# The second MLP product by Strassen's seven products instead of eight, in a two-layer hybrid decoder trunk

## Chip and metric

One core of a Trainium2 chip runs the whole program. The metric is device microseconds of one execution, median of the runs shown.

## What is computed

Two layers (DEPTH = 2) act on 512 tokens of 1024 features. Each layer normalises x, makes one wide input projection, runs three token mixers on its column groups (stick-breaking attention, sparse attention with a top-k indexer, a gated linear recurrence), merges them by sigmoid gates, projects the sum and adds it to x. Then comes the MLP:

```python
h2 = rms_norm(x, norm_mlp[l])
x = x + jnp.square(jax.nn.relu(h2 @ w_up[l])) @ w_down[l]
```

w_up is 1024 x 4096 and w_down is 4096 x 1024, all in float32.

## The kernel before

Activations lie with features on the 128 partitions and the 512 tokens along the free axis, so x is eight tiles of 128 x 512. Every main product is made in three passes for accuracy: each operand is cut into a high part (a copy in the reduced float32r format) and a low part (the remainder), and TensorE adds high x high, high x low and low x high into one PSUM bank. For weights, `split_weights` makes the high part on ScalarE and the remainder on VectorE, from a raw block of 1024 x 256 that one DMA on SP's queue has loaded into one of two raw buffers (N_RAW). High and low parts of weights have five buffers each (N_W); all activations share 76 tiles (N_T).

`fm` makes one output tile of 128 features: for each k-tile of 128 it issues the three matmuls of 512 columns. The MLP of a layer runs in four groups of 1024 hidden features. In group g the first product makes eight tiles u: `take_u` evicts a bank on VectorE with max(., 0) and the norm's factor, ScalarE squares it twice (into the high part and in place), VectorE makes the remainder. The second product (`rows_to_res`) takes 1024 rows of w_down in four column blocks of 256, that is two output tiles of eight k-tiles each, and `take_res` adds each finished bank to its tile of x on VectorE. In the last group `done` norms each x tile for the next layer (`norm_tile`) or sends it out.

The order of all instructions is fixed when the program is built. Operations are recorded first, each with a lane (main, prep for weights, norm, and one for each mixer: sb, idx, dsa, hg), a level and a planned duration; `order` then plays them forward on five engines. `choose` takes for each engine the ready operation with the earliest planned start and then the smallest level; AHEAD limits how far beyond the oldest open operation of a lane it may look; `of_banks` and `of_tiles` limit which lane may take a PSUM bank or a tile. ORDER_IN is the order of the input projection's column groups (h0 to h3, hv for the recurrence; iq and the tail of sv for the indexer; sqk and sv for the attention; dq for the sparse attention), ORDER_MIX the order in which the mixers are recorded, ORDER_OUT that of gates and branch projections. On the chip each engine runs its list in order.

In the profile nearly all engine operations carry the line of a helper: L586 for matmuls, L592 for transposes, L522 for everything on VectorE, ScalarE and GpSimd, L609 for DMAs. The tiles tell them apart: wr is a raw weight block, wh and wl its high and low parts, u, uh and ul the MLP's activations, pm the bank of a main product, zs and pi banks of the attention and the indexer.

Of the kernel before, what the change touches and what calls it, by code (L numbers as in the profile page):

```python
# [7 lines left out]
F32 = mybir.dt.float32  # L8
# [3 lines left out]
AF = mybir.ActivationFunctionType  # L12
# [4 lines left out]
P = 128  # L17
# [4 lines left out]
DEPTH = 2  # L22
# [19 lines left out]
LV_GATE = 1  # L42
SMALL = ("var", "rtok", "iw", "m8", "dss", "drs", "mn", "sm", "rc", "dec", "hrs")
ROOM = {"main": 12}
AHEAD = {"dsa": 80, "hg": 64, "idx": 160, "sb": 50}
BANKS = 4
BRANCHES = ("sb", "dsa", "hg")
ORDER_IN = ("h0", "h1", "h2", "h3", "hv", "iq", "sqk", "sv", "dq")
ORDER_MIX = ("sb", "index", "hgrn", "dsa_inputs", "dsa")
ORDER_OUT = (("gate", "sb", 0), ("gate", "sb", 1), ("gate", "dsa", 0), ("gate", "dsa", 1), ("branch", "sb", 0),  # L50
             ("gate", "hg", 0), ("gate", "hg", 1), ("branch", "dsa", 0), ("branch", "sb", 1), ("branch", "dsa", 1),
             ("branch", "hg", 0), ("branch", "hg", 1))
LEVELS = (4, 8, 16, 32)

# [160 lines left out]
class Program:  # L215
# [100 lines left out]
    def order(self, caps):  # L316
# [24 lines left out]
        avail = {e: [] for e in ENGINES}  # L341
# [5 lines left out]
        done, worked = [], {}  # L347
# [31 lines left out]
        def choose(e):  # L379
            c = clock[e]  # L380
            pick = None
            for o in avail[e]:
                if o.ready + SLACK[e] > c and pick is not None and pick[0][0] <= o.ready + SLACK[e]:
                    if pick[0][0] < o.ready + SLACK[e]:
                        continue
                if o.at - base[o.lane] >= AHEAD.get(o.lane, 1 << 30):
                    continue
                at = may(o)
                if at is None:
                    continue  # L390
                s = max(c, o.ready + SLACK[e], at)
                p = o.prio
                if e == "ACT" and o.acts and acts and o.acts != acts:
                    p = (p[0] + 3, p[1])
                key = (s, p)
                if pick is None or key < pick[0]:
                    pick = (key, o, max(c, o.ready, at))
            return pick

        while len(done) < len(self.ops):  # L400
# [6 lines left out]
            _, _, e = min(live)  # L407
            o, s = best[e][1], best[e][2]
# [3 lines left out]
            line, b = lanes[o.lane], base[o.lane]  # L412
            if o.at == b:
                while b < len(line) and line[b].gone:
                    b += 1
                base[o.lane] = b
                if o.lane in AHEAD:
                    stale |= set(ENGINES)
# [8 lines left out]
            us = o.us  # L427
# [4 lines left out]
            if e == "PE":  # L432
# [3 lines left out]
                w = int(s / SPAN)  # L436
# [16 lines left out]
            for t in o.tiles:  # L453
                t.left -= 1
                t.free_at = max(t.free_at, o.end)
                if not t.left and t.tag in free:
                    have = free[t.tag]
# [70 lines left out]
class Kernel:  # L528
# [224 lines left out]
    def tm(self, units, acts, n, consumer, tiles=range(NT)):  # L753

        banks = self.g.gang([self.ps("pm") for _ in tiles])
        k = 0
        for src in units:
            hi, lo = self.split_weights(src)
            c = hi.shape[1]
            self.on("main", 1)  # L760
            for bank, t in zip(banks, tiles):
                self.products(bank[:, 0:n], [(hi[:, i, :], lo[:, i, :]) for i in range(c)],
                              [tuple(x[:, P * t:P * (t + 1)] for x in acts[k + i]) for i in range(c)],
                              k == 0, k + c == ND, True)
            k += c
        self.on("main", 0)
        for bank, t in zip(banks, tiles):
            consumer(bank[:, 0:n], t)


    def begin_norm(self, gain0):
# [435 lines left out]
    def layer(self, l):  # L1207
        V = self.V
        L = {"hq": [], "hf": []}
        self.on("main", 0)  # L1210
        hid = self.hid
# [5 lines left out]
        w = self.w_in[l]  # L1217
# [52 lines left out]
        for s in ORDER_IN:  # L1270
            steps[s]()
        for s in ORDER_MIX:
            getattr(self, s)(L, l)
        self.on("main", 0)
        gates = {}
        mixed = [None] * ND
        final = []
# [19 lines left out]
        def branch(br, half):  # L1297
            wb = {"sb": self.w_sb, "dsa": self.w_dsa, "hg": self.w_hg}[br][l]
            ap = self.rows(wb, 512 * half, 512)
            r = self.load([(None, ap)], list(ap.shape))  # L1300
            for i in range(4):
                m = 4 * half + i
                t = gates.pop((br, m))

                def take_y(ps):
                    o = V.tensor_mul(t, t, ps)
                    if br == BRANCHES[-1] and m == 0:
                        L["late"] = [o]
                    if br == BRANCHES[0]:
                        mixed[m] = t  # L1310
                        return
                    V.tensor_add(mixed[m], mixed[m], t)
                    if br == BRANCHES[-1]:
                        hi, lo = self.r(name="mxh"), self.r(name="mxl")
                        self.split(hi, lo, mixed[m])
                        mixed[m] = None
                        final.append((hi, lo))

                self.fm([r[:, :, P * i:P * (i + 1)]], L["o_" + br], take_y)
# [19 lines left out]
        def rows_to_res(src, acts, after):  # L1339
            for c in range(4):  # L1340
                for j, u in enumerate(self.by_features(src, 256 * c)):
                    m = 2 * c + j
                    self.fm(u, acts, lambda ps: (take_res(ps, m), after(m)))

        rows_to_res(self.w_out[l], final, lambda m: self.norm_tile(m))
        hid = self.hid
        for g in range(4):
            self.on("main", 0)
            us = []

            def take_u(ps):
                t = self.f(name="u")
                V.scalar_tensor_tensor(t, ps, 0.0, self.rbc, op0=ALU.max, op1=ALU.mult)
                hi, lo = self.r(name="uh"), self.r(name="ul")
                self.act(hi, t, AF.Square)
                self.act(t, t, AF.Square)
                V.tensor_sub(lo, t, hi.bitcast(F32))
                us.append((hi, lo))

            for c in range(4):  # L1360
                for u in self.by_features(self.w_up[l], 1024 * g + 256 * c):
                    self.fm(u, hid, take_u)
            last = g == 3 and l + 1 < DEPTH
            if last:
                self.begin_norm(8 * (l + 1))
            def done(m):
                if last:
                    self.norm_tile(m, True)
                elif g == 3:
                    self.dma(self.out[P * m:P * (m + 1), :], self.xT[m])  # L1370

            rows_to_res(self.w_down[l][1024 * g:1024 * (g + 1), :], us, done)

    def run(self):
        V = self.V
# [22 lines left out]
def of_banks(lane, k, have, used, first):  # L1398
    n = lambda *lanes: sum(used.get(("ps", x), 0) for x in lanes)
    if lane == "main":  # L1400
        return n("main") + k <= BANKS
    if lane in ("norm", "out"):
        return True
    if not first or n("sb", "dsa", "idx", "hg") + k > 6:
        return False
    if lane in ("dsa", "idx"):
        return n("dsa", "idx") + k <= (3 if n("sb", "hg") else 6)
    return True
# [50 lines left out]
```

## Time and profile before

| | |
|---|---|
| median of 3 runs | 1719.15 us (1718.8 to 1719.84) |
| profiled execution | 1718.95 us, span of its instructions 1717.2 us |
| busy: TensorE, VectorE, ScalarE | 1675.1, 1025.6, 797.2 us |

The time of an execution is a little longer than the span between the first and the last profiled instruction. Busy times are unions of instructions; an instruction's duration can be longer than the time until the next one starts on the same engine, since they are pipelined.

### The profile page before, as it was taken

Reading aid. Unit: us, or ns where it says so; the run is one execution under the profiler, and the core shown is the slowest. Engines: PE = TensorE matmul, PEld = TensorE weight load, DVE = VectorE, ACT = ScalarE, POOL = GpSimd, SP = SyncE. Lnnn points to the kernel's source line nnn. Section 1 sums busy time; section 2 is a strip of 40 time slices with the busy share of each in tenths; the row PEclk is TensorE's granted clock in tenths of the full one; section 3 lists DMA queues with packets and bytes.
Section 4 is the critical chain, followed back from the end, with each engine's and each line's share of the span. In section 5 each row is a group of like instructions: output and inputs, shape, how many; then the busy total and the mean of one; then the engine's idle time right before and its main releaser. Section 6 shows DMA issues by size and latency. Waiting matters only on the chain.

```text
span 1717.2 us, 22265 instructions
## 1 busy us (share of the span) xinstructions
PE 1675.1 (98%) x8624; PEld 1364.9 (79%) x8624; DVE 1025.6 (60%) x2208; ACT 797.2 (46%) x1498; POOL 20.8 (1%) x12
## 2 busy tenths in 40 slices
PE   7999999998899999999999999999988999999999
PEld 6888887786688888888888888887766888888887
DVE  7545578996765443444564555699968643434342
ACT  6346867336444242324452568563464442424241
POOL 0000010000000000000000001000000000000000
PEclk9999999999999999999999999999999999999999
DMA  6222121220332323322432222212203323232322
GB/s 188 98 93 74 50 74 50 72 83 32 111 102 94 99 98 98 98 98 98 135 111 98 70 81 67 74 44 74 65 29 135 99 98 98 98 99 98 98 98 74
DMA packets 144154, 152.64 MB, mean 89 GB/s; under 512 B 5296, under 2 KB 128688, under 8 KB 144048
## 3 DMA queue, kind: packets, MB, share of 16 engines
q1 hardware_dynamic: 143328, 150.55, 27.0%
q8 instruction: 67, 1.10, 0.3%
q10 hardware_dynamic: 720, 0.68, 0.1%
q14 instruction: 39, 0.32, 0.1%
HBM read 147.02 MB, written 4.19 MB: 88 GB/s over the span
## 4 chain that ended last, share of the span: by engine, by line
PE 92%; DVE 5%; ACT 2%; issue 1%; DMA 0%; ACTq 0%; DVEq 0%
PE pm L586 82%; PE zs L586 3%; PE ph L586 2%; DVE gate L522 2%; PE po L586 1%; PE pd L592 1%; DVE wl L522 1%; PE pi L586 1%; DVE lg L522 1%; PE pd L586 1%; PE pt L592 1%; ACT lg L522 0%; DVE work L522 0%; DMA c2a<-in_cst_dram 0%; DVE mxl L522 0%
## 5 line engine op out<-in xcount | busy, mean ns | idle before, releaser
L522 ACT ACTIVATE wh<-wr 128x512 fp32r<-128x512 f32 (+3 forms) x552 | 336.9, 617 | 719.4 <-PE pm L586 699.3
L522 DVE TENSOR_TENSOR wl<-wr,wh 128x512 fp32r<-128x512 f32 (+3 forms) x552 | 362.0, 669 | 303.5 <-ACT wh L522 195.9
L586 PE MATMUL pm<-hh,wh 128*128 128x512 f32 x1120 | 392.8, 393 | 9.6 <-ACT wh L522 9.6
L586 PE MATMUL pm<-hh,wl 128*128 128x512 f32 x1120 | 395.3, 395 | 0.1
L586 PE MATMUL pm<-hl,wh 128*128 128x512 f32 x1120 | 393.9, 393 | 0.0
L586 PEld LDWEIGHTS pm<-hh,wh 128*128 128x128 f32 x1120 | 211.0, 188 | 52.9 <-ACT wh L522 9.6
L586 PEld LDWEIGHTS pm<-hh,wl 128*128 128x128 f32 x1120 | 210.8, 188 | 44.9 <-issue 1.4
L586 PEld LDWEIGHTS pm<-hl,wh 128*128 128x128 f32 x1120 | 211.0, 188 | 42.9 <-issue 0.5
L586 PE MATMUL pm<-ul,wh 128*128 128x512 f32 x512 | 179.7, 389 | 0.0
L586 PE MATMUL pm<-uh,wl 128*128 128x512 f32 x512 | 179.7, 389 | 0.0
L586 PE MATMUL pm<-uh,wh 128*128 128x512 f32 x512 | 179.7, 389 | 0.0
L522 DVE TENSOR_TENSOR x<-x,pm 128x512 f32<-128x512 f32 x80 | 54.9, 686 | 121.1 <-PE pm L586 120.4
L586 PEld LDWEIGHTS pm<-uh,wl 128*128 128x128 f32 x512 | 96.1, 188 | 20.1
L586 PEld LDWEIGHTS pm<-uh,wh 128*128 128x128 f32 x512 | 96.1, 188 | 19.9
L586 PEld LDWEIGHTS pm<-ul,wh 128*128 128x128 f32 x512 | 96.1, 188 | 19.9
L586 PE MATMUL pm<-wl,hh 128*128 128x512 f32 (+1 forms) x240 | 81.7, 386 | 0.0
L586 PE MATMUL pm<-wh,hl 128*128 128x512 f32 (+1 forms) x240 | 81.7, 388 | 0.0
L586 PE MATMUL pm<-wh,hh 128*128 128x512 f32 (+1 forms) x240 | 81.5, 387 | 0.0
L522 DVE SCALAR_TENSOR_TENSOR u<-pm,rbc 128x512 f32<-128x512 f32 x64 | 44.1, 690 | 57.3 <-PE pm L586 57.3
L522 DVE TENSOR_TENSOR ul<-u,uh 128x512 fp32r<-128x512 f32 x64 | 44.3, 693 | 38.9 <-ACT u L522 38.9
L522 ACT ACTIVATE uh<-u 128x512 fp32r<-128x512 f32 x64 | 40.2, 628 | 31.5 <-DVE u L522 31.5
L586 PEld LDWEIGHTS pm<-wl,hh 128*128 128x128 f32 x240 | 45.1, 188 | 8.2
(218 smaller groups left out, 2091.6 us busy)
## 6 DMA issues: line engine op xcount, KB each, us to landing
wr<-in_w_in_dram SPq DMA_DIRECT2D x42, 1024.0 KB, 5.0
wr<-in_w_up_dram SPq DMA_DIRECT2D x32, 1024.0 KB, 5.4
wr<-in_w_down_dram SPq DMA_DIRECT2D x32, 1024.0 KB, 5.2
wr<-in_w_in_dram SPq DMA_DIRECT2D x16, 512.0 KB, 5.4
wr<-in_w_out_dram SPq DMA_DIRECT2D x8, 1024.0 KB, 5.2
x<-in_x_dram SPq DMA_DIRECT2D x16, 256.0 KB, 5.6
wr<-in_w_in_dram SPq DMA_DIRECT2D x4, 768.0 KB, 4.3
wr<-in_w_br_sb_dram SPq DMA_DIRECT2D x4, 768.0 KB, 4.4
```

The lines of the kernel that those rows point to most:

```text
L522: return self._g.op(self._n, lambda: f(real(out), *[real(a) for a in args], **{k: real(a) for k, a in kw.items()}), outs, ins, us, acts, l ...
L586: return self.g.op("PE", lambda: nc.tensor.matmul(real(out), real(lhsT), real(rhs), start=start, stop=stop, **k), [out], [lhsT, rhs], us, ...
L592: return self.g.op("PE", lambda: nc.tensor.transpose(real(out), real(in_), real(ident)), [out], [in_, ident], us, kind=kind)
```

## The change

The second product is cut into 2 x 2 blocks: the two output tiles of a column block, even and odd k-tiles, and the two halves of 256 tokens. With four weight blocks and four activation blocks, Strassen's method (in Winograd's form) needs seven block products in place of eight, and sums of blocks before and after. `moving_seven` makes four differences for a pair of u tiles and splits seven activation blocks; `seven` makes four weight sums (s1 to s4), splits seven weight blocks, runs seven products of 4 k-tiles x 3 matmuls of 256 columns into three banks (x four times, y once, z twice, in the order x y x z x z x), and after each product adds the bank to one quarter of the two x tiles. All sums are on VectorE. The first column block of group g + 1's first product is recorded ahead of group g's second product. ORDER_IN, ORDER_MIX, ORDER_OUT and AHEAD change, and on TensorE `choose` prefers the oldest main operation that can start by the chosen one's time. SEVEN_OUT is False, so w_out's product stays as it is.

```diff
@@ -42,13 +42,15 @@
 LV_GATE = 1
 SMALL = ("var", "rtok", "iw", "m8", "dss", "drs", "mn", "sm", "rc", "dec", "hrs")
 ROOM = {"main": 12}
-AHEAD = {"dsa": 80, "hg": 64, "idx": 160, "sb": 50}
+AHEAD = {"dsa": 166, "hg": 163, "idx": 160, "sb": 17}
 BANKS = 4
+SEVEN_OUT = False
+LV_MOVE = 2
 BRANCHES = ("sb", "dsa", "hg")
-ORDER_IN = ("h0", "h1", "h2", "h3", "hv", "iq", "sqk", "sv", "dq")
-ORDER_MIX = ("sb", "index", "hgrn", "dsa_inputs", "dsa")
+ORDER_IN = ("sqk", "h0", "h1", "h2", "hv", "h3", "iq", "sv", "dq")
+ORDER_MIX = ("index", "hgrn", "sb", "dsa_inputs", "dsa")
 ORDER_OUT = (("gate", "sb", 0), ("gate", "sb", 1), ("gate", "dsa", 0), ("gate", "dsa", 1), ("branch", "sb", 0),
-             ("gate", "hg", 0), ("gate", "hg", 1), ("branch", "dsa", 0), ("branch", "sb", 1), ("branch", "dsa", 1),
+             ("gate", "hg", 0), ("branch", "sb", 1), ("gate", "hg", 1), ("branch", "dsa", 0), ("branch", "dsa", 1),
              ("branch", "hg", 0), ("branch", "hg", 1))
 LEVELS = (4, 8, 16, 32)
 
@@ -395,6 +397,14 @@
                 key = (s, p)
                 if pick is None or key < pick[0]:
                     pick = (key, o, max(c, o.ready, at))
+            if e == "PE" and pick is not None and pick[1].lane == "main":
+                o = pick[1]
+                for x in avail[e]:
+                    if x.lane == "main" and x.prio < o.prio and x.ready <= pick[2]:
+                        at = may(x)
+                        if at is not None and at <= pick[2]:
+                            o = x
+                pick = (pick[0], o, pick[2])
             return pick
 
         while len(done) < len(self.ops):
@@ -766,6 +776,78 @@
         self.on("main", 0)
         for bank, t in zip(banks, tiles):
             consumer(bank[:, 0:n], t)
+
+
+    def moving_seven(self, b0, b1):
+
+        V = self.V
+        h = lambda a, i: a[:, 256 * i:256 * (i + 1)]
+        ta, tb = self.f(name="ta"), self.f(name="tb")
+        V.tensor_sub(h(ta, 0), h(b0, 1), h(b0, 0))
+        V.tensor_sub(h(ta, 1), h(b1, 1), h(b0, 1))
+        V.tensor_sub(h(tb, 0), h(b1, 1), h(ta, 0))
+        V.tensor_sub(h(tb, 1), h(b1, 0), h(tb, 0))
+        out = {}
+        for src, names in ((h(b0, 0), ("b11",)), (b1, ("b21", "b22")), (tb, ("t2", "t4")), (ta, ("t1", "t3"))):
+            n = 256 * len(names)
+            hi, lo = self.r((P, n), "vh"), self.r((P, n), "vl")
+            self.split(hi, lo, src)
+            for i, k in enumerate(names):
+                out[k] = (h(hi, i), h(lo, i))
+        return out
+
+    def seven(self, src, moving, after):
+
+        V = self.V
+        for c in range(4):
+            ap = self.rows(src, 256 * c, 256)
+            r = self.load([(None, ap)], list(ap.shape)).rearrange("p (k s) c -> p k s c", s=2)
+            a = {(i, j): r[:, :, j, P * i:P * (i + 1)] for i in range(2) for j in range(2)}
+            self.on("prep", 1)
+            s1, s2, s3, s4 = (self.f((P, 4, P), "ws") for _ in range(4))
+            parts = {}
+
+            def cut(k, w):
+                parts[k] = self.split_weights(w)
+
+            cut("a11", a[0, 0])
+            cut("a12", a[0, 1])
+            self.on("prep", 1)
+            self.in_order(V.tensor_add(s1, a[1, 0], a[1, 1]), "last_sum")
+            self.in_order(V.tensor_sub(s2, s1, a[0, 0]), "last_sum")
+            cut("s2", s2)
+            cut("s1", s1)
+            self.on("prep", 1)
+            self.in_order(V.tensor_sub(s3, a[0, 0], a[1, 0]), "last_sum")
+            cut("s3", s3)
+            self.on("prep", 1)
+            self.in_order(V.tensor_sub(s4, a[0, 1], s2), "last_sum")
+            cut("s4", s4)
+            cut("a22", a[1, 1])
+            x = lambda i, j: self.xT[2 * c + i][:, 256 * j:256 * (j + 1)]
+            self.on("seven", 0)
+            banks = {k: self.ps("p" + k) for k in "xyz"}
+            first, order = set(), (("x", "a11", "b11", [(0, 0)]), ("y", "a12", "b21", [(0, 0)]),
+                                   ("x", "s2", "t2", [(0, 1)]), ("z", "s1", "t1", [(1, 1)]),
+                                   ("x", "s3", "t3", [(1, 1)]), ("z", "s4", "b22", [(0, 1)]),
+                                   ("x", "a22", "t4", [(1, 0)]))
+            for bank, w, b, into in order:
+                wh, wl = parts[w]
+                ps = banks[bank][:, 0:256]
+                self.on("main", 1)
+                n = len(moving)
+                for i in range(n):
+                    bh, bl = moving[i][b]
+                    for j, (p, q) in enumerate(((wh, bh), (wh, bl), (wl, bh))):
+                        self.mm(ps, p[:, i, :], q, bank not in first and i == 0 and j == 0, i == n - 1 and j == 2,
+                                skip_group_check=True)
+                first.add(bank)
+                self.on("seven", 0)
+
+                for at in into:
+                    V.tensor_add(x(*at), x(*at), ps)
+            after(2 * c)
+            after(2 * c + 1)
 
 
     def begin_norm(self, gain0):
@@ -1311,6 +1393,10 @@
                         return
                     V.tensor_add(mixed[m], mixed[m], t)
                     if br == BRANCHES[-1]:
+                        if SEVEN_OUT:
+                            if m % 2:
+                                final.append(self.moving_seven(mixed[m - 1], mixed[m]))
+                            return
                         hi, lo = self.r(name="mxh"), self.r(name="mxl")
                         self.split(hi, lo, mixed[m])
                         mixed[m] = None
@@ -1342,34 +1428,38 @@
                     m = 2 * c + j
                     self.fm(u, acts, lambda ps: (take_res(ps, m), after(m)))
 
-        rows_to_res(self.w_out[l], final, lambda m: self.norm_tile(m))
+        (self.seven if SEVEN_OUT else rows_to_res)(self.w_out[l], final, lambda m: self.norm_tile(m))
         hid = self.hid
-        for g in range(4):
-            self.on("main", 0)
-            us = []
-
+        us, moving = {g: [] for g in range(4)}, {g: [] for g in range(4)}
+
+        def up(g, c):
             def take_u(ps):
                 t = self.f(name="u")
                 V.scalar_tensor_tensor(t, ps, 0.0, self.rbc, op0=ALU.max, op1=ALU.mult)
-                hi, lo = self.r(name="uh"), self.r(name="ul")
-                self.act(hi, t, AF.Square)
                 self.act(t, t, AF.Square)
-                V.tensor_sub(lo, t, hi.bitcast(F32))
-                us.append((hi, lo))
-
-            for c in range(4):
-                for u in self.by_features(self.w_up[l], 1024 * g + 256 * c):
-                    self.fm(u, hid, take_u)
-            last = g == 3 and l + 1 < DEPTH
-            if last:
+                us[g].append(t)
+                if len(us[g]) % 2 == 0:
+                    self.on("main", LV_MOVE)
+                    moving[g].append(self.moving_seven(*us[g][-2:]))
+
+            self.on("main", 0)
+            for u in self.by_features(self.w_up[l], 1024 * g + 256 * c):
+                self.fm(u, hid, take_u)
+
+        def done(m):
+            if l + 1 < DEPTH:
+                self.norm_tile(m, True)
+            else:
+                self.dma(self.out[P * m:P * (m + 1), :], self.xT[m])
+
+        for g in range(4):
+            for c in range(1 if g else 0, 4):
+                up(g, c)
+            if g < 3:
+                up(g + 1, 0)
+            elif l + 1 < DEPTH:
                 self.begin_norm(8 * (l + 1))
-            def done(m):
-                if last:
-                    self.norm_tile(m, True)
-                elif g == 3:
-                    self.dma(self.out[P * m:P * (m + 1), :], self.xT[m])
-
-            rows_to_res(self.w_down[l][1024 * g:1024 * (g + 1), :], us, done)
+            self.seven(self.w_down[l][1024 * g:1024 * (g + 1), :], moving[g], done if g == 3 else lambda m: None)
 
     def run(self):
         V = self.V
@@ -1399,8 +1489,10 @@
     n = lambda *lanes: sum(used.get(("ps", x), 0) for x in lanes)
     if lane == "main":
         return n("main") + k <= BANKS
-    if lane in ("norm", "out"):
+    if lane == "norm":
         return True
+    if lane == "seven":
+        return have - k >= 1
     if not first or n("sb", "dsa", "idx", "hg") + k > 6:
         return False
     if lane in ("dsa", "idx"):
```

## Rows read from the trace of the kernel before

**Rows 1.** The page's busy time, share of the span and instructions of each engine.

```profile
span 1717.2 us, 22265 instructions
...
PE 1675.1 (98%) x8624; PEld 1364.9 (79%) x8624; DVE 1025.6 (60%) x2208; ACT 797.2 (46%) x1498; POOL 20.8 (1%) x12
```

**Rows 2.** The page's granted clock in 40 slices, 9 is full speed.

```profile
PEclk9999999999999999999999999999999999999999
```

**Rows 3.** Windows: stretch, then busy us (instructions) by engine, clock, DMA share, GB/s.

```profile
300.00:350.00 50.00, 48.15 (x308) 38.19 (x307) 50.00 (x143) 16.45 (x30) 0.00 (x0) 1.00 0.24 80
400.00:450.00 50.00, 42.44 (x281) 30.30 (x279) 31.47 (x101) 27.30 (x76) 0.00 (x0) 1.00 0.04 12
...
600.00:650.00 50.00, 50.00 (x222) 41.42 (x221) 24.26 (x37) 21.50 (x34) 0.00 (x0) 1.00 0.32 105
```

**Rows 4.** The chain that ended last: start, us, what (two longest pieces).

```profile
523.27 343.89 PE pm L586 x1517
...
1373.99 339.38 PE pm L586 x1497
```

**Rows 5.** Timeline of TensorE in the second product: start, us, instruction, count.

```profile
559.87 0.61 PE L586 MATMUL pm<-uh,wl 128*128 128x512 f32 x2
...
579.36 0.62 PE L586 MATMUL pm<-uh,wh 128*128 128x512 f32 x2
```

**Rows 6.** Timeline of TensorE in two bursts of the mixers, 256 columns.

```profile
136.44 0.28 PE L586 MATMUL zs<-sph,nones 128*128 128x256 f32 x1
136.45 0.19 PEld L586 LDWEIGHTS zs<-spl,nones 128*128 128x128 f32 x1
136.56 0.28 PE L586 MATMUL zs<-spl,nones 128*128 128x256 f32 x1
136.56 0.19 PEld L586 LDWEIGHTS zs<-sph,nones 128*128 128x128 f32 x1
...
136.68 0.22 PE L586 MATMUL zs<-sph,nones 128*128 128x128 f32 x1
...
272.62 0.28 PE L586 MATMUL pi<-ikh,iqT 128*128 128x256 f32 x1
...
272.85 0.40 PE L586 MATMUL pm<-hh,wh 128*128 128x512 f32 x1
```

**Rows 7.** Groups by form: busy us, mean ns of one, idle before and its releaser.

```profile
L522 DVE TENSOR_TENSOR wl<-wr,wh 128x512 fp32r<-128x512 f32 x488 | 329.6, 686 | 298.7 <-ACT wh L522 191.4 <-PE pm L586 106.8
L522 ACT ACTIVATE wh<-wr 128x512 fp32r<-128x512 f32 x488 | 305.5, 631 | 667.9 <-PE pm L586 650.6 <-ACT sq L522 4.0 <-DVE hq L522 4.0
...
L586 PE MATMUL pm<-uh,wl 128*128 128x512 f32 x512 | 179.7, 389 | 0.0
...
L522 DVE SCALAR_TENSOR_TENSOR u<-pm,rbc 128x512 f32<-128x512 f32 x64 | 44.1, 690 | 57.3 <-PE pm L586 57.3
L522 ACT ACTIVATE u<-u 128x512 f32<-128x512 f32 x64 | 40.5, 633 | 2.0
```

**Rows 8.** Timeline of VectorE in the mixers of both layers.

```profile
306.87 1.27 DVE L522 TENSOR_TENSOR wl<-wr,wh 128x512 fp32r<-128x512 f32 x2
308.07 0.68 DVE L522 MAX8 m<-work 128x8 f32<-128x512 f32 x1
...
1015.75 0.42 DVE L522 TENSOR_TENSOR st<-ikw,st 128x256 fp32r<-128x256 f32 x1
1016.09 0.28 DVE L522 SCALAR_TENSOR_TENSOR hst<-hst,f,ph 128x64 f32<-128x64 f32 x1
```

**Rows 9.** Timeline of ScalarE at the start.

```profile
8.96 1.15 ACT L522 ACTIVATE wh<-wr 128x512 fp32r<-128x512 f32 x2 [1.93 <-DMA wr<-in_w_in_dram]
```

**Rows 10.** The page's DMA issues: count, size, median us to landing.

```profile
wr<-in_w_down_dram SPq DMA_DIRECT2D x32, 1024.0 KB, 5.2
```

## The prediction

> **What bounds the kernel now.** I read the busy times first [rows 1]: TensorE is busy for 1675.1 of 1717.2 us, VectorE for 1025.6, ScalarE for 797.2. A busy TensorE need not be at its peak, so the clock comes next: full in all 40 slices [rows 2]. Then the stages [rows 3]: in the MLP (600 to 650 us) TensorE is busy for 50.00 of 50 us and VectorE for 24.26. In the mixers it is otherwise: from 300 to 350 us VectorE is the one with 50.00 of 50, and from 400 to 450 us TensorE is busy for only 42.44. The chain that ended last says the same [rows 4]: two pieces of 343.89 and 339.38 us, one for each layer's MLP, are matmuls and nothing else. So in the MLP a matmul saved is time saved, as long as VectorE, with about half of its time free there, can pay for it.
>
> **TensorE's gain.** The second product now has, for each of 2 layers, 4 groups and 4 column blocks, 2 output tiles x 8 k-tiles x 3 = 48 matmuls of 512 columns: 1536 in all, the 3 x 512 of [rows 7]. In [rows 5] the first and the last of 44 rows of two lie 19.49 us apart: 86 starts, 0.2266 us each. That is 348.1 us. After, a block has 7 products x 4 k-tiles x 3 = 84 matmuls of 256 columns, 2688 in all. Their spacing is seen in short bursts of the mixers [rows 6]: 136.44, 136.56, 136.68, so 0.12 us at two digits, each with a weight load of its own between; another two take from 272.62 to 272.85, 0.115 each. I take the mean, 0.118. 2688 x 0.118 = 317.2 us. The gain is 30.9 us, not the eighth of 348 (43.5), since a 256-column matmul costs 52% of a 512-column one. Taken at 0.116 or 0.12 it would be 36 or 26.
>
> A 256-column matmul leaves 0.118 us to hide a load that lasts 0.19 us in [rows 6]; two loads there start 0.11 us apart and delay nothing. The Trainium skill speaks against the change here: "TensorE: Matmul & The Clock Gate", section "Part 3: Packing small matmuls", says that a weight load overlaps running matmuls only where they use other row groups. All 128 rows of the array are in use here (128*128 in the lines), and yet the load is hidden, so this trace does not agree.
>
> **VectorE's price.** Each VectorE row lasts longer than it holds the engine. In [rows 8] two weight subtractions of 512 start at 306.87 and the next operation at 308.07: 0.60 each, where the mean duration is 0.686 [rows 7]. One of 256 holds it 0.34 (1015.75 to 1016.09). By these:
> A block of the product costs 4 weight remainders and 2 residual adds now, 6 x 0.60 = 3.6 us. After: 7 remainders and 4 weight sums of 512, and 7 adds of 256: 11 x 0.60 + 7 x 0.34 = 9.0 us. A pair of activation tiles costs 2 remainders now, 1.2 us; after, 4 differences and one remainder of 256 and three remainders of 512, 5 x 0.34 + 3 x 0.60 = 3.5 us. With 32 blocks and 32 pairs VectorE holds 32 x 5.4 + 32 x 2.3 = 246 us more. What hides it is TensorE's time in the same stage. For one group, the first product takes TensorE 192 x 0.2266 = 43.5 us, and VectorE 16 x 0.60 (weights) + 8 x 0.60 (evictions) + 4 x 3.5 = 28.4. The second takes TensorE 4 x 9.9 = 39.6 us and VectorE 4 x 9.0 = 36.0. VectorE goes from under half to 78% of the MLP and fits, but in the second product only by 0.9 us a block.
>
> ScalarE: two weight copies take 1.15 us [rows 9] where one lasts 0.631 [rows 7], so 0.52 each; 7 x 0.52 = 3.6 us a block, hidden under 9.9. DMA: the same 32 loads of 1 MB, 5.2 us each [rows 10], on the same queue, one a block of 9.9 us with two buffers; no cost. That the first block of group g+1's first product, with its load and its weight copies, is issued ahead of group g's second product moves work of the same kind, and gives 10.9 us of cover while the last pair of group g is split. The final output DMAs keep their number.
>
> **What is given back.** (a) VectorE runs in order, at 36 of 39.6 us, and gets 2 evictions of the next group besides. Where it comes late, a block stretches. Below, nothing: 3.6 us are left in each group (less than nothing is out, since work is only added). Above, the whole 31 us: then VectorE sets the pace. Of the rows, 300 to 350 us is the nearest, where VectorE is full and TensorE lacks 1.9 us of 50 [rows 3]; I take 1 us for each of the six groups that are followed by another: 6. (b) Group 3 of each layer has no next first product to cover its last pair. After the last matmul come eviction 0.69, square 0.63, copy 0.63, remainder 0.69 [rows 7] before the second of the seven products can use the tile, 2.6 us; TensorE has the first product (1.4 us) and three of four k-tiles of the second (1.1 us). With the differences of the pair behind it I take 1.5 us each: 3 (0 to 8). (c) In the first layer's group 3, eight tiles are normed for the next layer, at two VectorE operations a tile, 16 x 0.60 = 9.6 us upon 36.0, against 39.6: 6 us too much, of which 5 prepared weight parts (3.0 us of remainders) cover half. I take 4 (0 to 8). Together 13.
>
> **The order of the mixers** (input steps, mixer order, look-ahead, oldest main product first). It removes and adds no instruction. From 400 to 450 us TensorE lacks 7.6 us, in 300 to 350 us 1.9 [rows 3]; two layers have each. A better order could win up to about 16 us; widening the recurrence's window moves VectorE work out of 300 to 350 us, where the top-k chain needs it. A worse one can lose as much: the attention's window of 17 operations lets its chain run less far ahead, behind the values that come eighth in the input order, and then its VectorE work falls into that very stretch. Oldest-first gives up 0.25 us of planned slack at some switches. I take 0, with 16 either way.
>
> **Sum.** Against the profiled execution's own 1718.95 us (span 1717.2): 1718.95 - 30.9 + 13 + 0 = 1701. The median of the runs shown, 1719.15, is 0.2 above it, so 1701 it stays.
>
> **Rivals.**
> - *Little comes back.* The planned order keeps VectorE ahead and the mixers win some of their gap: 1719 - 31 + 3 - 6 = 1685. For it: 78% is not 100%. Against it: VectorE is in order and its margin is thin.
> - *The bank's hand-over decides: slower.* Four of seven sums stay in one PSUM bank (x): the next product into it may start only when VectorE has added the last one to the residual, and z has one such turn too: 4 turns a block, 128 in all. Between them lies one product, 12 x 0.118 = 1.42 us. The last matmul goes on for 0.16 us after the next has started (0.28 less 0.12 [rows 6]), the add lasts 0.42 (as the 256-column rows of [rows 8]): with one operation of 0.60 ahead of it that is 1.18 us, and it fits. With two ahead it is 1.78 and TensorE waits 0.36 us, 128 x 0.36 = 46 us: 1719 - 31 + 46 = 1734. It decides from a mean wait of 31/128 = 0.24 us on.
> - *The mixers' order loses.* The gap of 300 to 350 and 400 to 450 us doubles in both layers and 4 more us are given back in the MLP: 1701 + 16 + 4 = 1721; at half of that 1711.
> - *The weights don't hide.* Then each short matmul takes a load more. By rows, 0.118 + 0.11 (the loads' closest spacing, 136.45 to 136.56 [rows 6]) = 0.228, 2688 x 0.228 = 613 us against 348: 1984. That [rows 6] show the loads hidden leaves it 1 in 100. It is what the rule of the Trainium skill's page "TensorE: Matmul & The Clock Gate" named above would do.
> - *No change:* that VectorE sets the pace in the second product (term (a) at its upper end) with the mixers as they are: 1719.
>
> **How the numbers follow.** 0.2% (3.4 us) is about what a measurement of this kernel tells from no change. Chances: forecast 0.43, little comes back 0.25, mixers' order loses 0.14, hand-over 0.13, no change 0.04, weights 0.01. Faster is the first two and under half of the third, 0.74; same the fourth's small cases, the no-change case and part of the third, 0.09; slower 0.17. The likeliest case's own range is 1690 to 1712. The range must hold the first three: 1678 (the full gain, 1688, with 10 of the mixers) to 1722.
>
> **What would show it.** In the profile after: matmuls of 256 columns 0.117 to 0.12 us apart inside a product, with loads between; VectorE's busy share of the MLP's second product near 9 tenths and TensorE's near 10 in the first product; about 83 us for a pair of first and second products (87.0 now). TensorE's idle time before the x and z products, ended by VectorE's residual add, shows the hand-over; idle time ended by weight remainders shows (a); a hole of 1 to 4 us at the last group of each layer (b). The time up to the first MLP matmul of a layer (about 523 us now [rows 4]) shows the mixers' order by itself: it is predicted unmoved. The prediction is wrong if 256-column matmuls are further apart in long runs than in bursts of four, or if VectorE falls behind in its order.

## The result, and the profile after

The changed kernel takes 1672.49 us (median; 1670.55 to 1672.88), the kernel before 1718.97 in the same comparison: ratio 0.9728, 95% interval 0.9711 to 0.9744. That is 46.5 us faster; the forecast was 18, and the range ended at 1678. The profiled execution took 1672.88 us, its span 1671.1.

The page's busy times and the granted clock answer to [rows 1, 2]: VectorE rose from 60% to 76%, the clock stays up.

```profile
span 1671.1 us, 25574 instructions
...
PE 1643.0 (98%) x9776; PEld 1397.6 (84%) x9776; DVE 1272.7 (76%) x2784; ACT 879.9 (53%) x1653; POOL 21.4 (1%) x12
...
PEclk9999999999999999999999999999999999999999
```

The chain that ended last (start, us, what) answers to [rows 4]. The chain names a piece by its bank, so the long piece of each MLP is now cut where a second product writes px, py and pz (pieces of 12 or 24 matmuls, left out here). First products are still one piece (192 matmuls in 43.55 us), and from one to the next it is 83.99 us.

```profile
511.98 46.51 PE pm L596 x205
...
598.84 43.55 PE pm L596 x192
...
682.83 43.55 PE pm L596 x192
...
766.71 32.67 PE pm L596 x144
...
1339.32 46.51 PE pm L596 x205
```

The first pieces begin where a layer's first product does: at 511.98 and 1339.32 us, where it was 523.27 and 1373.99. So each execution can be cut into four stages. The cuts are the starts of VectorE's copy of the norm's factor (rbc), a few hundredths of a us from those pieces; the middle one is the layer boundary. Before:

```profile
523.31 0.69 DVE L522 COPY rbc<-pn 128x512 f32<-128x512 f32 x1 [1.64 <-PE pn L586]
...
873.09 0.69 DVE L522 COPY rbc<-pn 128x512 f32<-128x512 f32 x1 [0.41 <-PE pn L586]
...
1374.03 0.69 DVE L522 COPY rbc<-pn 128x512 f32<-128x512 f32 x1 [0.41 <-PE pn L586]
```

After:

```profile
512.02 0.69 DVE L532 COPY rbc<-pn 128x512 f32<-128x512 f32 x1 [1.40 <-PE pn L596]
...
851.71 0.69 DVE L532 COPY rbc<-pn 128x512 f32<-128x512 f32 x1 [1.41 <-PE pn L596]
...
1339.35 0.69 DVE L532 COPY rbc<-pn 128x512 f32<-128x512 f32 x1 [1.40 <-PE pn L596]
```

The stages in us:

```
                        mixers 1   MLP 1   mixers 2   MLP 2
before                    523.3    349.8     500.9    343.1
after                     512.0    339.7     487.6    331.7
difference                -11.3    -10.1     -13.3    -11.4
```

The MLP gained 21.5 us, near the 18 of the sum. The mixers, which were put at 0, gained 24.6. The cuts don't part the work quite alike: without the second products, the MLP stages start 767 and 728 main matmuls of 512 columns before and 768 and 732 after. For equal work (5 x 0.2266 = 1.1 us) the MLP gained 22.6 us and the mixers 23.5.

The windows (busy us and instructions of PE, PEld, DVE, ACT, POOL; clock, DMA share, GB/s) answer to [rows 3]. From 560 to 600 us a second product runs, from 602 to 642 a first one.

```profile
300.00:350.00 50.00, 48.52 (x310) 38.43 (x309) 50.00 (x135) 12.92 (x24) 0.00 (x0) 1.00 0.25 82
400.00:450.00 50.00, 50.00 (x294) 39.82 (x291) 34.91 (x89) 27.28 (x64) 0.00 (x0) 1.00 0.23 73
560.00:600.00 40.00, 40.00 (x330) 39.78 (x329) 36.65 (x73) 19.82 (x33) 0.00 (x0) 1.00 0.33 107
602.00:642.00 40.00, 40.00 (x179) 33.10 (x178) 29.88 (x54) 19.71 (x34) 0.00 (x0) 1.00 0.28 90
```

TensorE is never out of work in either, and VectorE has 92% and 75% to do. In the mixers VectorE is as full from 300 to 350 us as it was, but from 400 to 450 TensorE is busy throughout, where it had 42.44.

In the timeline, the first and the last of 48 matmuls of one second product lie 5.64 us apart: 47 steps, 0.120 us each, where the prediction took 0.118 from [rows 6].

```profile
565.52 0.28 PE L596 MATMUL pz<-vh,wh 128*128 128x256 f32 x1
...
571.16 0.28 PE L596 MATMUL py<-vh,wl 128*128 128x256 f32 x1
```

By groups (busy us, mean ns, idle before and its releaser), the hand-over of the bank cost next to nothing: TensorE waited 1.1 us for VectorE's add in the whole execution. The new remainders, sums and half adds on VectorE last what the rows they were costed by last (684 to 687 ns at 512 columns, 416 at 256).

```profile
L596 PE MATMUL px<-vh,wh 128*128 128x256 f32 x512 | 145.2, 284 | 1.1 <-DVE x L532 1.1
...
L532 DVE TENSOR_TENSOR wl<-ws,wh 128x512 fp32r<-128x512 f32 x128 | 87.7, 687 | 17.6 <-ACT wh L532 15.3
...
L532 DVE TENSOR_TENSOR x<-x,px 128x256 f32<-128x256 f32 x128 | 53.2, 416 | 10.2 <-PE px L596 7.5
...
L532 DVE TENSOR_TENSOR ws<-wr 128x512 f32<-128x512 f32 x64 | 43.8, 684 | 0.2 <-DMA wr<-in_w_down_dram 0.2
```

### The profile page after: what moved, and what is told of

Read it like the earlier page. It is cut to its first block, busy times and chain, and to the rows that moved or that the text cites. A ratio compares the mean times of both kernels' runs of the same rounds, so it can differ in the third digit from the quotient of the medians.

```text
span 1671.1 us, 25574 instructions
## 1 busy us (share of the span) xinstructions
PE 1643.0 (98%) x9776; PEld 1397.6 (84%) x9776; DVE 1272.7 (76%) x2784; ACT 879.9 (53%) x1653; POOL 21.4 (1%) x12
## 4 chain that ended last, share of the span: by engine, by line
PE 82%; DVE 12%; ACT 3%; POOL 1%; issue 1%; DMA 1%; SPq 0%; DVEq 0%
PE pm L596 56%; PE px L596 10%; PE pz L596 5%; PE py L596 2%; DVE wl L532 2%; PE zs L596 2%; DVE gate L532 2%; PE po L596 2%; PE ph L596 1%; DVE work L532 1%; DVE m L532 1%; PE pi L596 1%; PE pd L596 1%; PE pd L602 1%; DVE dq L532 1%
## 5 line engine op out<-in xcount | busy, mean ns | idle before, releaser
L532 DVE TENSOR_TENSOR wl<-wr,wh 128x512 fp32r<-128x512 f32 (+3 forms) x520 | 344.0, 667 | 134.4 <-ACT wh L532 124.9
L596 PE MATMUL px<-vh,wh 128*128 128x256 f32 x512 | 145.2, 284 | 1.1 <-DVE x L532 1.1
L596 PE MATMUL px<-vl,wh 128*128 128x256 f32 x512 | 145.0, 283 | 0.2
L596 PE MATMUL px<-vh,wl 128*128 128x256 f32 x512 | 144.5, 283 | 0.0
L532 ACT ACTIVATE wh<-ws 128x512 fp32r<-128x512 f32 x128 | 80.5, 631 | 111.2 <-PE px L596 46.6
L532 DVE TENSOR_TENSOR wl<-ws,wh 128x512 fp32r<-128x512 f32 x128 | 87.7, 687 | 17.6 <-ACT wh L532 15.3
L596 PEld LDWEIGHTS px<-vh,wh 128*128 128x128 f32 x512 | 98.1, 192 | 1.8 <-DVE x L532 0.9
L596 PEld LDWEIGHTS px<-vl,wh 128*128 128x128 f32 x512 | 98.2, 192 | 0.9 <-DVE vl L532 0.6
L596 PEld LDWEIGHTS px<-vh,wl 128*128 128x128 f32 x512 | 98.0, 192 | 0.0
L596 PE MATMUL pz<-vh,wh 128*128 128x256 f32 x256 | 72.7, 284 | 0.0
L596 PE MATMUL pz<-vl,wh 128*128 128x256 f32 x256 | 72.4, 283 | 0.0
```

The source lines that it names most:

```text
L532: return self._g.op(self._n, lambda: f(real(out), *[real(a) for a in args], **{k: real(a) for k, a in kw.items()}), outs, ins, us, acts, l ...
L596: return self.g.op("PE", lambda: nc.tensor.matmul(real(out), real(lhsT), real(rhs), start=start, stop=stop, **k), [out], [lhsT, rhs], us, ...
```

## Experiments

In what follows "the orders" are ORDER_IN, ORDER_MIX and ORDER_OUT, "the look-ahead" is AHEAD (hg is the recurrence's limit, sb the attention's, dsa the sparse attention's), and "the rule" is that TensorE takes the oldest main operation first.

**Where a stage loses time.** A TensorE that counts as busy may still stand half empty between matmuls. So for each matmul I also took the time until the next one starts, less columns / 2.4 GHz plus 13.3 ns (which is the 226.6 ns measured at 512 columns and the 120 at 256; for short ones 110 ns, the loads' spacing in [rows 6], is taken as the least). Below, "lost by starts" is the sum of all such excesses of more than 30 ns. Mixers are cut at the start of the top-k search, the first softmax operation of the sparse attention and the last part of its output. "Main matmuls" are those of the bank pm within the sparse attention: they are its cover, other work for TensorE while the sparse attention's own chain waits. Each cell has layer 1 and layer 2, in us:

```
                          stage        to search   to sparse  in sparse    after it   main
                                                   attention  attention               matmuls
before                 491.7 500.9    11.9 11.9    4.4  6.2   17.5 15.7    5.2  6.1    61  72
after                  479.4 487.6    13.4 13.6    4.3  4.3    6.6  6.6    5.0  4.8   168 168
orders only (e1)       478.7 488.2    13.4 13.7    4.3  4.3    6.6  6.6    4.3  5.4   168 168
rule alone (e6)        502.0 511.4    21.4 23.8    5.7  4.6   16.6 15.7    6.1  7.3    58  58
look-ahead alone (e8)  506.2 498.8    12.3 12.6   13.3 11.6    9.7  9.4   17.4  5.9   152 136
no rule (e5)           509.4 493.5    13.4 12.4   13.4 11.8    6.9  7.7   20.9  5.3   150 184
old look-ahead (e7)    505.1 516.6    21.6 23.0    4.1  3.1   21.5 21.5    5.8  8.9    46  46
recurrence's old (e10) 500.0 505.9    15.2 15.4    3.7  3.0   21.5 21.4    7.6  5.7    46  46
attention's old (e11)  480.0 496.6    14.4 21.8    3.7  3.4    6.4  6.2    5.3  6.3   167 158
old input order (e12)  487.1 487.5    19.5 13.3    4.1  4.3    7.0  6.6    6.3  5.1   140 168
163 alone (e13)        492.7 506.3    15.6 16.6    9.9 10.6    7.9 11.5    6.0  7.8   185 161
163, rule (e14)        499.0 494.3    22.3 11.4    3.5 11.6   14.7  6.6    7.2  6.0   124 169
163, rule, input (e15) 486.4 506.7    14.4 22.8    3.7  3.4   10.9 13.4    6.7  7.3   134 124
```

(Stages of layer 1 run here from the copy of the first norm's factor, at about 32 us.)

**The two halves apart.** One run takes the orders, the look-ahead and the rule without the seven products, one the seven products without them.

```diff
 # e1: before.py
-AHEAD = {"dsa": 80, "hg": 64, "idx": 160, "sb": 50}
+AHEAD = {"dsa": 166, "hg": 163, "idx": 160, "sb": 17}
+            if e == "PE" and pick is not None and pick[1].lane == "main":
 ...
 # and ORDER_IN, ORDER_MIX, ORDER_OUT of after.py; e2: after.py with all of these undone
```

> The kernel before with the new input order, mixer order, output order, look-ahead and the oldest-first rule, and with the old eight-product MLP. If the orders by themselves shorten the mixers, the two mixer stages fall from 523 and 501 us to about 512 and 488, the MLP stages stay at 350 and 343, and the time is 1719 - 25 = 1694 us. If the mixers gain only together with the seven products, it stays within 5 us of 1719.

1693.43 us, ratio 0.9853 (0.9838 to 0.9867): stages 508.9, 350.0, 488.2, 344.0. Orders, look-ahead and rule shorten the mixers without the seven products.

> The kernel after with all orders, the look-ahead and the choice rule of before: the seven products alone. If the two halves of the change are independent, the MLP stages are about 340 and 332 us, the mixers stay at 523 and 501, and the time is 1719 - 21 = 1698 us. If the seven products also bring the mixers' gain, it is near 1673.

1719.84 us, ratio 1.0002 (0.9993 to 1.0012): stages 526.1, 353.8, 499.6, 342.0. That was neither: alone the seven products gain nothing. Something in the other half is needed for them.

**What the seven products need.** Two runs: after without the rule, and before with nothing but the rule.

```diff
 # e5: after.py (e6 adds the same lines to before.py)
-            if e == "PE" and pick is not None and pick[1].lane == "main":
-                o = pick[1]
-                for x in avail[e]:
-                    if x.lane == "main" and x.prio < o.prio and x.ready <= pick[2]:
...
```

> The kernel after without the oldest-first rule on TensorE, all else kept. If the rule is what lets the seven products gain, the MLP stages go back from 340 and 332 to about 354 and 342 us (as with the seven products alone), and the time is 1672 + 24 = 1696 us or more. If it was the orders and the look-ahead that did it, or the rule matters only in the mixers, the MLP stages stay at 340 and 332.

1728.45 us, ratio 1.0051 (1.0034 to 1.0067); MLP stages 353.7 and 341.0. So the rule decides the MLP. The timeline of TensorE shows what it does there: without it, a block product (256 columns) takes turns with a product of the next group (512 columns), matmul by matmul, and further on three or four block products with each other.

```profile
579.46 0.28 PE L588 MATMUL px<-vh,wh 128*128 128x256 f32 x1
579.58 0.40 PE L588 MATMUL pm<-hl,wh 128*128 128x512 f32 x1
579.81 0.28 PE L588 MATMUL px<-vl,wh 128*128 128x256 f32 x1
579.93 0.40 PE L588 MATMUL pm<-hh,wl 128*128 128x512 f32 x1
580.17 0.28 PE L588 MATMUL px<-vh,wl 128*128 128x256 f32 x1
...
588.24 0.28 PE L588 MATMUL pz<-vh,wl 128*128 128x256 f32 x1
588.36 0.28 PE L588 MATMUL px<-vh,wl 128*128 128x256 f32 x1
589.05 0.38 PE L588 MATMUL px<-vh,wh 128*128 128x256 f32 x1 [0.41 <-ACT wh L524]
```

The turns themselves cost nothing (0.12 us to the next start behind 256 columns, 0.23 to 0.24 behind 512); the waits do. In the stretch of the first MLP, TensorE stood idle for 3.8 us before the first matmuls of a k-tile into x, mostly for weight parts:

```profile
L588 PE MATMUL px<-vh,wh 128*128 128x256 f32 x256 | 69.5, 289 | 3.8 <-ACT wh L524 2.9 <-DVE x L524 0.6
```

Lost by starts, it is more: 14.6 and 10.6 us in the two stages, for 3.0 and 0.7 after, and 7.6 and 5.1 of that ended with ScalarE's copy of a weight part. The two stages are 14 and 9 us longer than after. That products kept open side by side come to their ends together, and hold weight buffers and banks for longer, is an argument; the runs show the interleaving, the waits and the price.

> The kernel before with the oldest-first rule and nothing else. If the rule matters only where short products wait for VectorE, the MLP stages stay at 350 and 343 us and the time at 1719. If it also gives the mixers their gain, the mixer stages fall from 523 and 501 to 510 and 488 and the time to 1694.

1736.99 us, ratio 1.0105 (1.009 to 1.012); MLP stages 350.0 and 344.0, mixers 532.5 and 511.4. In the old MLP the rule is worth nothing, and in the old mixers it costs 20 us.

A third run gives the rule to the MLP's operations alone (they are marked when recorded), with all orders of before:

```diff
 # e9: after.py with ORDER_IN, ORDER_MIX, ORDER_OUT and AHEAD of before.py
-            if e == "PE" and pick is not None and pick[1].lane == "main":
+            if e == "PE" and pick is not None and pick[1].lane == "main" and pick[1].mlp:
```

> The kernel before with the seven products and the oldest-first rule for the MLP's products alone; orders, look-ahead and the choice in the mixers are those of before. If the seven products gain 22 us as soon as TensorE finishes one block product before the next, the MLP stages are 340 and 332 us, the mixers 523 and 501 from the time's start, and the time is 1719 - 22 = 1697 us. If the MLP's gain hangs on the look-ahead or the orders, it is near 1720, as with the seven products alone.

1700.56 us, ratio 0.989 (0.9873 to 0.9906); stages 522.9, 342.4, 500.4, 332.0. It differs from the seven products alone by the rule in the MLP, and is 19 us faster. It comes out at the forecast, in part by luck. Its MLP stages gain 18.5 us but hold 17 more main matmuls than before (780 and 732 for 767 and 728), so for equal work they gain 22.4; and the mixers are not left as they were: layer 2 loses 43.0 us by starts in them, for 39.9.

**What sets the spacing of 0.120 us.**

```diff
 # e3: after.py
-                        self.mm(ps, p[:, i, :], q, bank not in first and i == 0 and j == 0, ...
+                        e = 256 if bank not in first and i == 0 and j == 0 else 240
+                        self.mm(ps[:, 0:e], p[:, i, :], q[:, 0:e], bank not in first and i == 0 and j == 0, ...
```

> The kernel after, but of each block product all matmuls except the first into a bank leave out the last 16 of their 256 columns (that part of the sums is not computed). If the spacing of short matmuls is columns / 2.4 GHz plus a fixed 13.3 ns, as 226.6 ns for 512 columns would have it, it falls from 120 to 113.3 ns, a block of 84 from 10.1 to about 9.6 us, and the time by about 16 us to 1656. If the weight load sets the spacing, it stays at 120 ns and 1672 us.

1654.68 us, in one run of a kernel that leaves out 16 of 256 columns. The timeline has ten steps in 1.12 us, 0.112 each:

```profile
566.76 0.27 PE L596 MATMUL py<-vl,wh 128*128 128x240 f32 x1
...
567.88 0.28 PE L596 MATMUL py<-vh,wl 128*128 128x240 f32 x1
```

The columns set it; at 256 the weight load is still hidden.

**The same in the output projection.** `SEVEN_OUT = True`, nothing else.

> The kernel after with the output projection of the mixers made by seven products as well. If TensorE is its bound too, each layer's projection falls from 32 k-tile pairs at 226.6 ns (43.5 us) to four blocks of 10.1 us (40.3), and the time by 6 us to about 1666. If VectorE, which is full there while it merges the gates, must make the differences first, the start of the projection waits for them and the time is 1672 to 1680.

1700.32 us, ratio 0.9893 (0.9878 to 0.9907), 28 us worse than after: mixers 523.3 and 502.5, MLP as after. The windows and the groups of the first layer's merge show why: VectorE is full in both windows (24.97 of 25 us each, where after has 23.64 and 19.63 in the same two), TensorE waits for the activations' and the weights' parts (vh, vl, wh), and with TensorE busy for 17 to 20 of 25 us the granted clock is 0.68 in the mean of the second window, so most of that window ran at the lower of its two levels (1.2 GHz for 2.4). It is the second case, but beyond its 1680. After the sparse attention 22.5 and 22.9 us are lost by starts, for 5.0 and 4.8.

```profile
430.00:455.00 25.00, 19.81 (x91) 15.98 (x89) 24.97 (x50) 10.10 (x21) 0.00 (x0) 0.97 0.42 148
455.00:480.00 25.00, 17.02 (x78) 15.00 (x79) 24.97 (x50) 9.23 (x16) 0.00 (x0) 0.68 0.25 84
```

```profile
L596 PE MATMUL px<-vh,wh 128*128 128x256 f32 x12 | 4.3, 360 | 4.9 <-ACT wh L532 3.5 <-ACT vh L532 1.4
L596 PE MATMUL px<-vl,wh 128*128 128x256 f32 x12 | 4.1, 343 | 1.6 <-DVE vl L532 1.6
```

**Which edit moved the mixers.**

```diff
 # e7: after.py, look-ahead of before
-AHEAD = {"dsa": 166, "hg": 163, "idx": 160, "sb": 17}
+AHEAD = {"dsa": 80, "hg": 64, "idx": 160, "sb": 50}
 # e10: only "hg": 64; e11: only "sb": 50; e12: only ORDER_IN of before.py; e8: before.py with the new AHEAD
```

> The kernel after with the look-ahead limits of before. If the look-ahead makes the mixers' gain, the mixer stages go back to 523 and 501 us and the time to 1697; if the input, mixer and output orders make it, they stay at 512 and 488 and the time at 1672.

1725.9 us, ratio 1.0038 (1.0022 to 1.0053).

> The kernel before with the new look-ahead limits and nothing else. If these make the mixers' gain, 1694 us; if they need the new orders, 1719 or worse.

1728.31 us, ratio 1.0056 (1.0039 to 1.0073). Undone, the look-ahead costs more than the whole gain; alone, it costs too.

> The kernel after with the recurrence's look-ahead of before (64 for 163). If that limit moves the recurrence's end and with it the cover of the sparse attention, TensorE's loss in the sparse attention goes from 6.6 back to about 20 us in each layer, the recurrence ends before it starts, and the time is 1715 or more. If the attention's limit (17 for 50) does it, the loss stays at 6.6 and the time at 1672.

1709.82 us, ratio 0.9942 (0.9922 to 0.9962): 21.5 and 21.4 us lost in the sparse attention, 46 main matmuls there for 168. It is the recurrence's limit that makes the cover. The windows are the whole of layer 1's sparse attention, before, after and in this run:

```profile
389.90:442.50 52.60, 44.21 (x294) 30.84 (x292) 32.45 (x112) 34.98 (x89) 0.00 (x0) 1.00 0.08 26
```

```profile
367.00:430.70 63.70, 63.28 (x393) 49.08 (x392) 39.67 (x127) 41.19 (x100) 0.00 (x0) 1.00 0.16 51
```

```profile
396.30:449.20 52.90, 41.08 (x274) 28.82 (x272) 27.92 (x105) 33.19 (x85) 0.00 (x0) 0.97 0.03 11
```

> The kernel after with the attention's look-ahead of before (50 for 17). The counterpart of the last run: if the attention's limit makes the cover, the loss in the sparse attention goes to about 20 us a layer and the time to 1715; if the recurrence's does, it stays at 6.6 there, and only the start up to the top-k search changes, by 10 us a layer or less.

1681.94 us, ratio 0.978 (0.9761 to 0.98). The cover stays (6.4, 6.2); in layer 2 the stretch up to the search loses 21.8 for 13.6.

> The kernel after with the input order of before (the recurrence's columns first, the attention's seventh). If the attention's columns at the head fill the stretch up to the top-k search, the loss there goes from 13.4 us to about 22 a layer, as in the two runs that had the rule without the orders, and the time to 1690. If the order of gates and branches does that, it stays at 1672.

1680.36 us, ratio 0.9771 (0.9751 to 0.979). Here it is layer 1 that loses 19.5 for 13.4 up to the search.

Then the recurrence's limit on the kernel before, alone, with the rule, and with the rule and the new input order:

```diff
 # e13, e14, e15: before.py
-AHEAD = {"dsa": 80, "hg": 64, "idx": 160, "sb": 50}
+AHEAD = {"dsa": 80, "hg": 163, "idx": 160, "sb": 50}
 # e14 and e15: the rule as well; e15: ORDER_IN of after.py as well
```

> The kernel before with the recurrence's look-ahead at 163 and nothing else. If this limit alone makes the cover, TensorE's loss in the sparse attention falls from 17 to below 10 us a layer. If the wide window also lets the recurrence end so late that the merge waits for it (without the oldest-first rule), 15 us or more come back after the sparse attention or between search and attention, and the time is 1719 or more; if not, it is near 1697.

1723.67 us, ratio 1.0029 (1.0015 to 1.0042). Half expected: the cover comes (17.5 to 7.9 in layer 1), and is lost again, but between the start and the sparse attention (16 to 17 before the search, 10 to 11 after it), not in the merge.

> The kernel before with that limit and the oldest-first rule. If the rule brings the open main products to their end in turn and so takes away the late merge, the loss after the attention goes back to about 5 us and the time is below 1710; the loss up to the search stays near 20 us, since the input order is the old one. If the rule does nothing for it, 1719 or more.

1718.69 us, ratio 0.9988 (0.9977 to 1.0), nearly the second case. But in layer 1 the stretch from search to sparse attention is mended and the one up to the search is not; in layer 2 it is the other way round.

> The kernel before with that limit, the rule and the new input order. If these three make the mixers' gain, 1694 us, as with all order edits together. If the output order or the attention's limit is needed too, 1705 or more.

1720.05 us, ratio 1.0012 (1.0001 to 1.0023). Three edits don't make the gain: layer 2 loses 22.8 us up to the search, and the sparse attention 10.9 and 13.4, for 6.6. Some of what is still missing there (the limits of the two attentions, the mixer order, the output order) is needed too; of these only the attention's limit had a run of its own (e11).

## Why the prediction was off

**The step that failed** is "The order of the mixers ... I take 0, with 16 either way." It measured 24.6 us (23.5 for equal work), beyond its own bound, and the range's end at 1678 left the mixers only 10. Two things were wrong in it. The bound was taken from idle time: 7.6 us from 400 to 450 and 1.9 from 300 to 350 [rows 3] (two layers of that would be 19, not 16). But in the whole of the sparse attention TensorE was idle for 8.4 of 52.6 us by its busy time, and lost 17.5 by its starts. Short matmuls count as busy to their modelled ends (0.28 us at 256 columns, where the next can start after 0.12), and hide it. The weight loads tell: busy for 30.84 of 52.60 us there (59%), for 83% in the MLP [rows 3], and for 49.08 of 63.70 (77%) after. The Trainium skill's page "Perfetto Trace Analysis", section "Identifying the Most-Contended Engine", says just this, that matmul busy time is no measure of distance from the peak and the weight loads' busy share is a better one; the trace agrees.

And the mechanism was told the wrong way round. Widening the recurrence's window was to take VectorE work out of 300 to 350 us, where the top-k search needs it; that stretch is as full as it was, and the search, from its start to that of the sparse attention, takes as long (87.1 us for 87.4 in layer 1). What happened is that the search starts 24 us earlier (247.2 for 270.9 us after the norm), while the last split of the recurrence's output ends 46 us later (408.7 for 363.0) and the last of the gates' products is evicted 33 us later (392.5 for 359.9); the recurrence's state steps end where they did (321.2 for 319.2). So 168 main matmuls are left to fill the sparse attention, for 61. In every run with the limit at 163 the loss there is 6.2 to 14.7 us, in every run with 64 it is 15.7 to 21.5. That took 11 and 9 us out of 12 and 13 (all four stretches of the table together lose 10 and 11 us less). Without some of the other edits it is lost again in front of the sparse attention or, in layer 1 of e5 and e8, behind it. Why the plan puts off the recurrence's output with a wider window, and why edits that win together cost 4 to 18 us singly, the runs don't show. That the attention's limit (e11) and the input order (e12) each move mainly one layer says that the plan's result is no sum of its edits.

**Oldest-first** was costed at "0.25 us of planned slack at some switches" and put with the mixers. It is what the MLP's gain hangs on: 1719.8 without, 1700.6 with the rule there. The prediction assumed that block products run one after the other, and no row of before could show it, since products of 512 columns gain nothing from it.

**TensorE's gain** was the right mechanism, its size a little high: 30.9 us at 0.118, and 348.1 - 2688 x 0.120 = 25.5 at the measured spacing. Bursts of two or three were too short to take the last 2% from.

**What is given back** was 13 us in the sum and is 4 by the stages (25.5 less 21.5), 2.9 for equal work (25.5 less 22.6). (a), 6: nothing, VectorE at 92% kept up. (b), 3: 1.3 us lost by starts, about 0.7 at the last group of each layer. (c), 4: about 1.6 us, of which the two waits of the timeline, for VectorE's add in the group that norms, are 1.1:

```profile
826.38 0.36 PE L596 MATMUL px<-vh,wh 128*128 128x256 f32 x1 [0.46 <-DVE x L532]
...
834.70 0.38 PE L596 MATMUL px<-vh,wh 128*128 128x256 f32 x1 [0.66 <-DVE x L532]
```

The gain was taken 5.4 us too high and what is given back 10 us too high. That the MLP comes out near the forecast, 22.6 for 18, is in part luck: two errors that work against each other.

**VectorE's price** was right: 36.0 of 39.6 us foreseen for the second product (91%), 36.65 of 40 seen; busy time rose by 247.1 us, 246 foreseen. So was a pair of products: 83 foreseen, 84.0 seen.

**The rivals.** The hand-over waited twice, 1.1 us in all, far below 0.24 us in each of 128 turns; its arithmetic held (1.18 us fit into 1.42). That it turns at two operations ahead was not tried. The weights hide. The mixers' order was the open term; the only case that let the mixers win anything, "little comes back", gave them 6.

## What to carry to other kernels

Bound what a reordering can give by the spacing of matmul starts or the weight loads' share of a stretch, not by idle time. When a product is cut into shorter ones that hand buffers to each other, look first at the order in which the open ones are worked off: one after the other can be the whole gain. And where one change alters an algorithm and a planner's constants, predict them apart, with a wide range for the constants: here all of them together took 26 us off the kernel before (e1), and the rule alone added 18 (e6).

## What the runs showed of the hardware

In long runs reduced-float32 matmuls start 226.6 ns apart at 512 columns and 120.0 at 256: both are columns at 2.4 GHz plus 13.3 ns. At 240 columns it is 112, slightly below the 113.3 of that line. A full-array weight load before each of them, 0.19 us long by the profile, was hidden in all three.
